# One-hot gate operands in an expert-retrieval kernel: made dense, token by token, by compare-and-scale instructions instead of for four interleaved tokens at once

## The chip, the core and the metric

The kernel runs on one core of a Trainium2 chip. Five engines work side by side, each with an in-order queue: TensorE (PE in the profile; its weight loads are listed as PEld), VectorE (DVE), ScalarE (ACT), GpSimd (POOL) and SyncE (SP, which issues the DMAs). They wait for each other through semaphores. The metric is the device time of one execution in microseconds (us); less is better.

## What is computed

The model is a decoder trunk of two layers on 256 tokens of width 1024. Each layer has a token-mixing sublayer (recurrent, state-space and attention heads; not touched here) and an expert retrieval, which is the place of the change. For each token, eight heads each choose 16 of 128 x 128 = 16384 experts; an expert is a pair of keys (i, j) and has a softmax gate. The output is the gated sum of the chosen experts:

```python
idx = jnp.take_along_axis(cand_i.reshape(c, PEER_HEADS, -1), best_pos, axis=-1)
gate = jax.nn.softmax(best_s, axis=-1)
ue = u[idx]
ve = v[idx]
act = jax.nn.gelu(jnp.einsum('td,thkd->thk', xc, ue).astype(jnp.float32), approximate=False)
return jnp.einsum('thk,thkd->td', (gate * act).astype(xc.dtype), ve)
```

## The kernel before

The kernel does not gather experts. It multiplies the tokens with all 16384 rows of u (the *first product*), applies GeLU, multiplies by a gate that is zero for the experts not chosen, and multiplies with all rows of v (the *second product*). The weights stream from HBM in pieces of 128 x 1024 floats. Each piece is split into a high half `hi` by ACT (line 117) and a low half `lo` by DVE, or for about every third piece of u by POOL (line 118), and every product is made of three matmuls: hi x hTh, hi x hTl, lo x hTh. All matmuls outside the transposes are issued by the helper `mm`, so they stand on line 193 in the profile; they are told apart by their tiles.

In `peer`, the loop over `jp_` (64 rounds, two pieces of u each) does the first product into the PSUM tile `acc`, 24 matmuls of 256 columns for one piece (columns are tokens). Between the pieces, `bg.step` advances background work that is written as Python generators: first `routing` for the two halves of the tokens, which finds the chosen keys and leaves them as `ijT` (key numbers i and j, in half floats) and `gT` (the gate as a high and a low half float); partition = choice (head and rank, 128 of them), column = token. Then `wgen` runs, one group of TG = 4 tokens for one piece of u, 64 groups for a layer. In a step it calls `gates` for group g, `wmm` for group g - 1 and `apply` for group g - 2.

`gates` makes the operands of a group on DVE in three instructions. Line 937 compares a constant ramp with the keys i and j of four tokens (`eq`, 1024 elements a partition). Line 940 multiplies the i half by the two gate halves (the first two planes of `ga`). Line 942 scales the j half for the low plane (the third plane of `ga`). The four tokens are the innermost dimension of these tiles, so the 128 elements that belong to one token lie four elements apart. `wmm` then makes the dense 128 x 128 gate matrix of each token from two half-float matmuls of 128 columns, 8 matmuls for a group. `apply` puts the gates onto `act`: for the experts whose first product is already there by a multiplication on DVE (line 956), for the others by a copy on ACT (line 958). `uevac` (lines 977 to 980) takes each finished `acc` through GeLU.

The order of instructions on each engine is fixed when the program is built, by a scheduler that goes by its own estimate of when operands are ready; on the chip each engine then follows its list. `eq` and `ga` have two buffers each. All of this happens twice, once per layer; in the first layer the groups are worked on from about 431 to 677 us, in the second from about 1474 to 1720 us.

Of the kernel before, what the change touches and what calls it, by code (L numbers as in the profile page):

```python
# [10 lines left out]
F16 = mybir.dt.float16  # L11
U32 = mybir.dt.uint32
AF = mybir.ActivationFunctionType
OP = mybir.AluOpType
AX = mybir.AxisListType

D = 1024
# [29 lines left out]
def trunk(ctx, tc, x, wst, ut, vr, pp_d, rb_d, lnrow, bd_d, keys_d, out):  # L47
    nc = tc.nc
    PE, ACT, DVE, POOL, SP = nc.tensor, nc.scalar, nc.vector, nc.gpsimd, nc.sync

    const = ctx.enter_context(tc.tile_pool(name="const", bufs=1))
    hpool = ctx.enter_context(tc.tile_pool(name="hpool", bufs=1))
    stream = ctx.enter_context(tc.tile_pool(name="stream", bufs=1))
    psum = ctx.enter_context(tc.tile_pool(name="psum", bufs=1, space=bass.MemoryType.PSUM))
    dram = ctx.enter_context(tc.tile_pool(name="dram", bufs=1, space=bass.MemoryType.DRAM))

# [1 line left out]
    items = []  # L58
    index = {}

# [70 lines left out]
    def rawtile(key):  # L131
        n = index[key]
        pump_dma()
        return raws[n]

    def rawdone(key):
        n = index[key]
        raws.pop(n)
        done.add(n)
        pump_dma()  # L140


# [1 line left out]
    mixp = tc.tile_pool(name="mix0", bufs=1)  # L144
    mix = mixp.__enter__()
    jp = mix.tile([128, 128], F32, name="jp")
    POOL.iota(jp, pattern=[[1, 128]], base=0, channel_multiplier=-1, allow_small_or_imprecise_dtypes=True)
    ident = const.tile([128, 128], F32, name="ident")
    POOL.tensor_scalar(ident, jp, 0.0, None, op0=OP.is_equal)
    iota4 = const.tile([128, 128, 4], F16, name="iota4")  # L150
    iota16 = const.tile([128, 16, 16], BF16, name="iota16")
    identb = const.tile([128, 128], BF16, name="identb")
    tri_le = const.tile([128, 128], F32, name="tri_le")
# [14 lines left out]
        return rb[:, l, o:o + w]  # L168

    def make_consts():  # L170
        POOL.iota(iota4, pattern=[[1, 128], [0, 4]], base=0, channel_multiplier=0, allow_small_or_imprecise_dtypes=True)
        POOL.iota(iota16, pattern=[[1, 16], [0, 16]], base=0, channel_multiplier=0, allow_small_or_imprecise_dtypes=True)
        POOL.tensor_scalar(identb, jp, 0.0, None, op0=OP.is_equal)
        POOL.tensor_scalar(tri_le, jp, 0.0, None, op0=OP.is_ge)
        POOL.tensor_scalar(tri_gt, jp, 0.0, None, op0=OP.is_lt)
        POOL.tensor_scalar(tri_gr, jp, 0.0, None, op0=OP.is_lt)
        for i in range(4):
            POOL.tensor_scalar(mask0[:, i, :], jp, 0.0, NEG, op0=OP.is_gt, op1=OP.mult)
        for i in range(2):
            POOL.tensor_scalar(mask1[:, i, 0, :], jp, 0.0, NEG, op0=OP.is_le, op1=OP.mult)  # L180
            POOL.tensor_scalar(mask1[:, i, 1, :], jp, 0.0, NEG, op0=OP.is_gt, op1=OP.mult)
# [10 lines left out]
    def mm(ps, lhsT, rhs, start, stop):  # L192
        PE.matmul(ps, lhsT, rhs, start=start, stop=stop)  # L193
# [4 lines left out]
    def acc_bank():  # L198
        return psum.tile([128, 512], F32, name="acc", bufs=4)

# [1 line left out]
    def layer_norm(h, pool, pre, gb, store, nxt=None, final=False, after=None):  # L202
        """h [128, 2, D] in place, stored to store; returns the transposed split operands."""
        ring = isinstance(gb[0], tuple)
        g, b = (rawtile(k) for k in gb) if ring else gb
        with tc.high_priority():
            hT = layer_norm_(h, pool, pre, g, b, store, nxt and index[nxt], final, after)
        for k in gb if ring else ():
            rawdone(k)
        return hT  # L210
# [93 lines left out]
    def seq(t):  # L304
        return [(w[0],) + tuple(int(ch) for ch in w[1:]) for w in t.split()]

    # (step, token block, part): r residual and sums, m mean and squares, v variance, n reciprocal root, s centre and
    # gain, o scale and bias with the transposes, l low halves, p the next weight pieces
    LN_ORDER = (
        seq("r00 r01 m0 v0 s00 s01 n00 r10 n01 r11 n02 m1 n03 v1 o00 o01 s10 n10 s11 n11 l00 n12 p1 n13 o10 o11 l01 l10 l11 p2"),  # L310
        seq("r00 r01 m0 s00 s01 v0 r10 n00 r11 n01 m1 n02 n03 o00 v1 o01 s10 n10 s11 n11 n12 n13 p1 o10 o11 l00 l01 l10 l11 p2"),
        seq("r00 r01 m0 s00 s01 v0 n00 n01 n02 r10 n03 r11 m1 s10 s11 v1 o00 n10 o01 n11 n12 n13 o10 o11"))

# [1 line left out]
    class Background:  # L315
        def __init__(self):
            self.q = []
# [39 lines left out]
        return y  # L357

    def log1p_exp_neg_abs(pool, o, xin, n, tag):
        """o = max(x, 0) + log1p(exp(-|x|)) on [128, n]"""  # L360
        a = pool.tile([128, n], F32, name=tag + "_a")
        e = pool.tile([128, n], F32, name=tag + "_e")
        q = pool.tile([128, n], F32, name=tag + "_q")
        ACT.activation(a, xin, AF.Abs)
        ACT.activation(e, a, AF.Exp, scale=-1.0)
        DVE.tensor_scalar(a, e, 2.0, None, op0=OP.add)
        DVE.reciprocal(a, a)
        DVE.tensor_tensor(e, e, a, op=OP.mult)
        DVE.tensor_tensor(a, e, e, op=OP.mult)
        DVE.tensor_scalar(q, a, 1.0 / 17.0, None, op0=OP.mult)  # L370
        for c in (15, 13, 11, 9, 7, 5, 3):
            DVE.scalar_tensor_tensor(q, q, 1.0 / c, a, op0=OP.add, op1=OP.mult)
        DVE.scalar_tensor_tensor(q, q, 1.0, e, op0=OP.add, op1=OP.mult)
        DVE.tensor_scalar(o, xin, 0.0, None, op0=OP.max)
        DVE.scalar_tensor_tensor(o, q, 2.0, o, op0=OP.mult, op1=OP.add)

# [1 line left out]
    def layer_consts(l, mix):  # L378
        av = mix.tile([128, 16], F32, name="av")
        sp4 = mix.tile([128, 4], F32, name="sp4")  # L380
        sp8 = mix.tile([128, 4], F32, name="sp8")
        sp2 = mix.tile([128, 4], F32, name="sp2")
        hba = mix.tile([128, 8], F32, name="hba")
        lamn = mix.tile([128, 4], F32, name="lamn")
        ACT.activation(av, RB("alog", l), AF.Exp)
        DVE.tensor_scalar(lamn, P("lam", l, 0, 4), -1.0, None, op0=OP.mult)
        log1p_exp_neg_abs(mix, sp8, lamn, 4, "lm")
        DVE.tensor_scalar(sp2, sp8, 2.0, None, op0=OP.mult)
        DVE.tensor_scalar(sp4, sp8, -4.0, None, op0=OP.mult)
        DVE.tensor_scalar(hba, P("rba", l, 0, 8), 0.5, None, op0=OP.mult)  # L390
        return av, sp2, sp4, hba

    def mixer(l, mix, h, hT, pre):
# [3 lines left out]
        yTl = mix.tile([128, 16, SEQ], F32R, name="yTl")  # L397
        xs = mix.tile([128, N_XBC, SEQ], F32, name="xs")

        # small per-layer values  # L400
        dt = mix.tile([128, 2, 16], F32, name="dt")
        da = mix.tile([128, 2, 16], F32, name="da")
        das = mix.tile([128, 2, 2, 16], F32R, name="das")
# [25 lines left out]
            yield  # L429
            yield  # L430

        # causal depthwise convolution
        def conv(o, xp, w0, bias=None):
            if bias is None:
                DVE.tensor_scalar(o, xp[:, 0:SEQ], w0(0), None, op0=OP.mult)
# [157 lines left out]
        ii = mix.tile([128, 4, SEQ], F32, name="ii")  # L593
# [129 lines left out]
                stages[st_](*units[u])  # L723
                yield

        # projection schedule
        order = [8, 9, 10, 11, 0, 1, 2, 3, 4, 5, 6, 7]
        for n, blk in enumerate(order):
            ps = bank([128, SEQ])
# [5 lines left out]
            if n == 3:  # L735
                ps = bank([128, SEQ])
# [8 lines left out]
        for blk in range(4):  # L745
            ps = bank([128, SEQ])
# [6 lines left out]
        for blk in range(4):  # L753
            ps = bank([128, SEQ])
# [5 lines left out]
        for i in range(6):  # L760
            ps = bank([128, SEQ])
# [7 lines left out]
        for nh in range(2):  # L769
            pz = [acc_bank() for _ in range(2)]  # L770
            for kp in range(4):
                hi, lo = weights(("w", l, n0 + nh * 4 + kp))
                for kk in range(2):
                    k = kp * 2 + kk
                    cs = slice(kk * 512, (kk + 1) * 512)
                    for tb in range(2):
                        ts = slice(tb * 128, (tb + 1) * 128)
# [6 lines left out]
                ACT.activation(sz[:, tb, nh * 512:(nh + 1) * 512], pz[tb], AF.Silu)  # L784
        n0 += N_Z
        bg.add(ssm_final())
        # output projection
        po = [[acc_bank() for _ in range(2)] for _ in range(2)]
        oorder = list(range(0, 16))
        def out_mm(i, kb, w, tb):  # L790
# [26 lines left out]

    RA, RB2, RX = 2, 2, 1

# [1 line left out]
    def peer(l, pool, hT):  # L821
        hTh, hTl = hT
        act = pool.tile([128, 128, SEQ], F32, name="act")
        ijT = pool.tile([128, 2, SEQ], F16, name="ijT")
        gT = pool.tile([128, 2, SEQ], F16, name="gT")
# [5 lines left out]
        for hh in range(8):  # L831
            ps = bank([128, SEQ])
# [3 lines left out]
        for tb in range(2):  # L836
            for hp in range(4):
                ps = bank([128, 2, 256])
# [13 lines left out]
        def routing(tb):  # L852
            base = 92
# [13 lines left out]
            gr = view(base + 7, 1)[:, 128:256]  # L867
# [37 lines left out]
            ts = slice(tb * 128, (tb + 1) * 128)  # L905
            for i in range(2):
# [9 lines left out]
                ps = bank([128, 128])  # L916
# [4 lines left out]
            ps = bank([128, 128])  # L921
# [1 line left out]
            yield  # L923
            ACT.activation(gT[:, 0, ts], ps, AF.Copy, scale=GS)
            DVE.scalar_tensor_tensor(gr, ps, GS, gT[:, 0, ts], op0=OP.mult, op1=OP.subtract)
            ACT.activation(gT[:, 1, ts], gr, AF.Copy, scale=LS)
            yield

        state = dict(c=0, t=0)
        TG = 4  # L930
        GS, LS = float(2 ** 15), float(2 ** 11)

        def gates(t0):
            eq = pool.tile([128, 2, 128, TG], F16, name="eq", bufs=2)
            A = pool.tile([128, 3, 128, TG], F16, name="ga", bufs=2)
            sh = [128, 2, 128, TG]
            DVE.tensor_tensor(eq, iota4[:, None, :, :].to_broadcast(sh),  # L937
                              ijT[:, :, None, t0:t0 + TG].to_broadcast(sh), op=OP.is_equal)
            # gate = (hi + lo / LS) / GS in half floats
            DVE.tensor_tensor(A[:, 0:2], eq[:, 0:1].to_broadcast(sh), gT[:, :, None, t0:t0 + TG].to_broadcast(sh),  # L940
                              op=OP.mult)
            DVE.tensor_scalar(A[:, 2], eq[:, 1], 1.0 / LS, None, op0=OP.mult)  # L942
            return A, eq

        def wmm(A, eq):
            ps = bank([128, TG, 128])
            for i in range(TG):
                mm(ps[:, i, :], A[:, 0, :, i], eq[:, 1, :, i], True, False)
                mm(ps[:, i, :], A[:, 1, :, i], A[:, 2, :, i], False, True)
            return ps  # L950

        def apply(t0, ps):
# [34 lines left out]
        for jp_ in range(64):  # L987
            ps = psum.tile([128, 2, SEQ], F32, name="acc", bufs=4)
# [3 lines left out]
            uevac(jp_, ps)  # L992
        bg.drain()

        # second product
        po = [[acc_bank() for _ in range(2)] for _ in range(2)]
        early = [[pool.tile([128, w], F32R, name=nm, bufs=2)[:, 0:2 * SEQ] for _ in range(2)]
                 for nm, w in (("eq", 512), ("ga", 768))]
# [37 lines left out]
                v_mm(j, w, tb)  # L1036
        return po

# [1 line left out]
    h = mix.tile([128, 2, D], F32, name="h")  # L1040
    gb = mix.tile([128, 2, D], F32, name="y")
    for i in range(2):
# [8 lines left out]
    for l in range(DEPTH):  # L1051
# [12 lines left out]
        h = mix.tile([128, 2, D], F32, name="h")  # L1064
# [85 lines left out]
```

## Time and profile before

| | |
|---|---|
| time, median of 3 runs | 2103.36 us (2100.47 to 2103.9) |
| profiled execution, first to last instruction | 2106.6 us |
| PE, PEld busy | 2030.2 us (96%), 1835.5 us (87%) |
| DVE busy | 1548.2 us (73%) |
| ACT, POOL busy | 1062.8 us (50%), 238.3 us (11%) |
| mean granted TensorE clock | 0.991 of full speed |
| DMA | 344.84 MB, 164 GB/s |

The profiled execution is not one of the three timed runs: the profile gives its own time as its span, 2106.6 us, and no other. Busy shares are averages over stages in which different engines set the pace, so the stage of the change has to be looked at by itself. A busy PE in this profile means that some matmul was in flight; since matmuls overlap, the distance from one start to the next tells more than a duration.

### The profile page before, as it was taken

The page shows a single profiled execution, that of the slowest core. Times are in us where ns is not written, and L with a number is a line of the kernel's source. Part 1 is how long each engine was busy: PE and PEld are TensorE (multiplying, and loading weights), DVE is VectorE, ACT ScalarE, POOL GpSimd, SP SyncE. Part 2 cuts the span into 40 slices and gives each one's busy share as a digit, 9 for nine tenths or more (in the row PEclk, how much of TensorE's full clock was granted, in tenths as well). Part 3 has the DMA queues.
Part 4 walks back from the last instruction along what each step waited for, and adds up shares of the span by engine and source line. Part 5 has one row for each costly group of instructions (what it writes and reads, how often), then busy time and mean ns, then how long its engine had stood idle before and what let it go on. Part 6 is the DMA issues. An engine that isn't in the chain of part 4 may idle for free. (4 is left out here: it accounts for less than half of the span.)

```text
span 2106.6 us, 33808 instructions
## 1 busy us (share of the span) xinstructions
PE 2030.2 (96%) x13212; PEld 1835.5 (87%) x13212; DVE 1548.2 (73%) x2713; ACT 1062.8 (50%) x1523; POOL 238.3 (11%) x120
## 2 busy tenths in 40 slices
PE   7999889999999999999989999899999999999998
PEld 6887889999999888888888769899999998888886
DVE  8786697379999655555687867963999995555555
ACT  5576455454443544444566755554444344444444
POOL 3100122222220000000010001222222200000000
PEclk9999999999999999999999999999999999999999
DMA  6434445544434666666654335455444446666665
GB/s 206 136 110 150 152 152 168 180 141 140 132 130 135 195 194 194 192 194 195 197 180 139 108 133 170 155 173 174 140 132 134 136 151 190 193 196 192 195 195 170
DMA packets 95919, 344.84 MB, mean 164 GB/s; under 512 B 11680, under 2 KB 11952, under 8 KB 95760
## 3 DMA queue, kind: packets, MB, share of 16 engines
q1 hardware_dynamic: 95552, 342.27, 50.3%
q8 instruction: 103, 1.69, 0.3%
q0 software_dynamic: 208, 0.42, 0.1%
q14 instruction: 56, 0.46, 0.1%
HBM read 339.51 MB, written 3.15 MB: 163 GB/s over the span
## 5 line engine op out<-in xcount | busy, mean ns | idle before, releaser
L118 DVE TENSOR_TENSOR lo<-raw,hi 128x1024 fp32r<-128x1024 f32 x544 | 677.5, 1246 | 383.9 <-ACT hi L117 383.5
L117 ACT ACTIVATE hi<-raw 128x1024 fp32r<-128x1024 f32 x630 | 663.8, 1056 | 452.2 <-PE acc L193 342.5
L193 PE MATMUL acc<-hTh,lo 128*128 128x256 f32 x2048 | 581.8, 284 | 20.1 <-DVE lo L118 18.8
L193 PE MATMUL acc<-hTh,hi 128*128 128x256 f32 x2048 | 592.0, 289 | 0.2 <-ACT hi L117 0.2
L193 PE MATMUL acc<-hTl,hi 128*128 128x256 f32 x2048 | 580.1, 283 | 0.0
L193 PEld LDWEIGHTS acc<-hTh,lo 128*128 128x128 f32 x2048 | 392.1, 191 | 24.3 <-DVE lo L118 22.4
L193 PE MATMUL acc<-hi,hTl 128*128 128x512 f32 x1056 | 411.4, 390 | 0.0
L193 PE MATMUL acc<-hi,hTh 128*128 128x512 f32 x1056 | 411.2, 390 | 0.0
L193 PE MATMUL acc<-lo,hTh 128*128 128x512 f32 x1056 | 411.1, 389 | 0.0
L193 PEld LDWEIGHTS acc<-hTh,hi 128*128 128x128 f32 x2048 | 394.3, 193 | 0.7 <-ACT hi L117 0.4
L193 PEld LDWEIGHTS acc<-hTl,hi 128*128 128x128 f32 x2048 | 392.8, 192 | 0.1
L118 POOL TENSOR_TENSOR lo<-raw,hi 128x1024 fp32r<-128x1024 f32 x86 | 223.6, 2602 | 1046.7 <-ACT hi L117 1015.7
L193 PEld LDWEIGHTS acc<-hi,hTh 128*128 128x128 f32 x1056 | 198.3, 188 | 41.6 <-issue 0.7
L193 PEld LDWEIGHTS acc<-hi,hTl 128*128 128x128 f32 x1056 | 198.2, 188 | 41.1
L193 PEld LDWEIGHTS acc<-lo,hTh 128*128 128x128 f32 x1056 | 198.3, 188 | 41.1
L193 PE MATMUL w<-hTh,hi 128*128 128x256 f32 x560 | 161.4, 299 | 7.5 <-DVE y L495 5.7
L1011 ACT ACTIVATE hTh<-act 128x512 fp32r<-128x512 f32 x124 | 77.7, 631 | 166.2 <-PE acc L193 166.2
L1012 DVE TENSOR_TENSOR hTl<-act,hTh 128x512 fp32r<-128x512 f32 x124 | 85.4, 693 | 97.4 <-ACT hTh L1011 97.4
L193 PE MATMUL w<-hTh,lo 128*128 128x256 f32 x560 | 156.9, 289 | 0.0
L193 PE MATMUL w<-hTl,hi 128*128 128x256 f32 x560 | 155.4, 287 | 0.0
L958 ACT ACTIVATE act<-w 128x272 f32<-128x272 f32 (+32 forms) x128 | 61.1, 478 | 146.5 <-DVE act L956 145.8
L193 PE MATMUL w<-eq,ga 128*128 128x128 f16 x512 | 128.0, 294 | 6.9 <-DVE ga L940 6.9
(268 smaller groups left out, 2323.5 us busy)
## 6 DMA issues: line engine op xcount, KB each, us to landing
raw<-in_ut SPq DMA_DIRECT2D x256, 512.0 KB, 3.5
raw<-in_vr SPq DMA_DIRECT2D x256, 512.0 KB, 3.5
raw<-in_wst SPq DMA_DIRECT2D x118, 512.0 KB, 3.5
raw<-in_lnrow SPq DMA_DIRECT2D x8, 512.0 KB, 3.6
hd<-h SPq DMA_DIRECT2D x4, 512.0 KB, 3.9
raw<-hd SPq DMA_DIRECT2D x4, 512.0 KB, 3.5
h<-in_x SPq DMA_DIRECT2D x2, 512.0 KB, 5.7
y<-in_lnrow SPq DMA_DIRECT2D x2, 512.0 KB, 7.0
```

Of the source, the lines that this page charges most:

```text
L117: ACT.activation(hi, raw, AF.Copy)
L118: (POOL if n in on_pool else DVE).tensor_tensor(lo, raw, hi.bitcast(F32), op=OP.subtract)
L193: PE.matmul(ps, lhsT, rhs, start=start, stop=stop)
L958: ACT.activation(v[:, :, c:128], ps[:, :, c:128], AF.Copy, scale=1.0 / GS)
L1011: ACT.activation(gh, src, AF.Copy)
L1012: DVE.tensor_tensor(gl, src, gh.bitcast(F32), op=OP.subtract)
```

## The change

`gates` now loops over the four tokens of a group. For each token it makes one row of `eq` (the key j) and two rows of `ga` (the key i, scaled by the high and by the low half of the gate), each 128 elements that lie side by side, and each by one tensor-scalar instruction on DVE. The instruction compares the ramp with a key that it reads per partition and, for `ga`, multiplies by a gate half that it reads per partition. The ramp shrinks from 512 to 128 elements, the scale `LS` of the low half goes, and with it the third plane of `ga`. `wmm` issues as many matmuls as before, on the dense rows. The other lines of the diff remove comments, so that later lines have numbers that are one less.

```diff
-    iota4 = const.tile([128, 128, 4], F16, name="iota4")
+    iota1 = const.tile([128, 128], F16, name="iota1")
...
-        POOL.iota(iota4, pattern=[[1, 128], [0, 4]], base=0, channel_multiplier=0, allow_small_or_imprecise_dtypes=True)
+        POOL.iota(iota1, pattern=[[1, 128]], base=0, channel_multiplier=0, allow_small_or_imprecise_dtypes=True)
...
-            ACT.activation(gT[:, 1, ts], gr, AF.Copy, scale=LS)
+            ACT.activation(gT[:, 1, ts], gr, AF.Copy)
...
         def gates(t0):
-            eq = pool.tile([128, 2, 128, TG], F16, name="eq", bufs=2)
-            A = pool.tile([128, 3, 128, TG], F16, name="ga", bufs=2)
-            sh = [128, 2, 128, TG]
-            DVE.tensor_tensor(eq, iota4[:, None, :, :].to_broadcast(sh),
-                              ijT[:, :, None, t0:t0 + TG].to_broadcast(sh), op=OP.is_equal)
-            DVE.tensor_tensor(A[:, 0:2], eq[:, 0:1].to_broadcast(sh), gT[:, :, None, t0:t0 + TG].to_broadcast(sh),
-                              op=OP.mult)
-            DVE.tensor_scalar(A[:, 2], eq[:, 1], 1.0 / LS, None, op0=OP.mult)
+            eq = pool.tile([128, TG, 128], F16, name="eq", bufs=2)
+            A = pool.tile([128, TG, 2, 128], F16, name="ga", bufs=2)
+            for i in range(TG):
+                ii, jj = (ijT[:, c, t0 + i:t0 + i + 1] for c in range(2))
+                DVE.tensor_scalar(eq[:, i, :], iota1, jj, None, op0=OP.is_equal)
+                for c in range(2):
+                    DVE.tensor_scalar(A[:, i, c, :], iota1, ii, gT[:, c, t0 + i:t0 + i + 1], op0=OP.is_equal, op1=OP.mult)
             return A, eq
 
         def wmm(A, eq):
             ps = bank([128, TG, 128])
             for i in range(TG):
-                mm(ps[:, i, :], A[:, 0, :, i], eq[:, 1, :, i], True, False)
-                mm(ps[:, i, :], A[:, 1, :, i], A[:, 2, :, i], False, True)
+                for c in range(2):
+                    mm(ps[:, i, :], A[:, i, c, :], eq[:, i, :], c == 0, c == 1)
             return ps
```

The next two lists are DVE's order in the middle of the first layer's groups, around the two multiplications by the gates (`apply`) that cover 78 experts a token; `iota_78` is the ramp. Before:

```order
L937 TENSOR_TENSOR eq<-iota_78,ijT 128x1024
L118 TENSOR_TENSOR lo<-raw,hi 128x1024
L978 TENSOR_TENSOR act<-act,acc 128x2x92
L940 TENSOR_TENSOR ga<-eq,gT 128x1024
L942 TENSOR_SCALAR ga<-eq 128x512
L956 SCALAR_TENSOR_TENSOR act<-w,act 128x4x78
L937 TENSOR_TENSOR eq<-iota_78,ijT 128x1024
L118 TENSOR_TENSOR lo<-raw,hi 128x1024
L940 TENSOR_TENSOR ga<-eq,gT 128x1024
L942 TENSOR_SCALAR ga<-eq 128x512
L956 SCALAR_TENSOR_TENSOR act<-w,act 128x4x78
```

And at the same place after the change:

```order
L118 TENSOR_TENSOR lo<-raw,hi 128x1024
L977 TENSOR_TENSOR act<-act,acc 128x2x92
L939 TENSOR_SCALAR eq<-iota_78,ijT 128x128
L941 TENSOR_SCALAR ga<-iota_78,ijT,gT 128x128 x2
L939 TENSOR_SCALAR eq<-iota_78,ijT 128x128
L941 TENSOR_SCALAR ga<-iota_78,ijT,gT 128x128 x2
L939 TENSOR_SCALAR eq<-iota_78,ijT 128x128
L941 TENSOR_SCALAR ga<-iota_78,ijT,gT 128x128 x2
L939 TENSOR_SCALAR eq<-iota_78,ijT 128x128
L941 TENSOR_SCALAR ga<-iota_78,ijT,gT 128x128 x2
L955 SCALAR_TENSOR_TENSOR act<-w,act 128x4x78
L118 TENSOR_TENSOR lo<-raw,hi 128x1024
```

Between two `apply` steps there are now twelve instructions with one or two per-partition operands where there were three without any; the split of a weight piece, the multiplication after GeLU and `apply` keep their places between the groups.

On PE the same stretch is, before, a block of eight gate matmuls between the 24 matmuls of one piece and those of the next (its last rows here):

```order
L193 LDWEIGHTS ga
L193 MATMUL w<-eq,ga 128x128
L193 LDWEIGHTS ga
L193 MATMUL w<-ga 128x128
L193 MATMUL acc<-hTh,hi 128x256
L193 MATMUL acc<-hTl,hi 128x256
L193 MATMUL acc<-hTh,lo 128x256
```

And after the change:

```order
L193 LDWEIGHTS ga
L193 MATMUL w<-eq,ga 128x128
L193 MATMUL acc<-hTh,hi 128x256
L193 LDWEIGHTS ga
L193 MATMUL w<-eq,ga 128x128
L193 MATMUL acc<-hTl,hi 128x256
L193 MATMUL acc<-hTh,lo 128x256
L193 MATMUL acc<-hTh,hi 128x256
L193 LDWEIGHTS ga
L193 MATMUL w<-eq,ga 128x128
```

From about the eighteenth group of a layer on, the gate matmuls are scattered singly between those of the first product. Of the first product's 3072 matmuls in a layer, 216 come after the last gate matmul, where it was 240: 24 matmuls, one piece of u, more are done by then.

## Rows read from the trace of the kernel before

**Rows 1.** The page: its first line, the span.

```profile
span 2106.6 us, 33808 instructions
```

**Rows 2.** Windows: start:end length, PE, PEld, DVE, ACT, POOL busy (count), clock, DMA, GB/s.

```profile
431.00:677.00 246.00, 242.26 (x2016) 237.32 (x2014) 234.82 (x323) 108.12 (x186) 48.52 (x18) 1.00 0.41 134
1474.00:1720.00 246.00, 242.86 (x2024) 238.12 (x2022) 234.46 (x323) 108.51 (x186) 49.36 (x18) 1.00 0.41 135
```

**Rows 3.** Groups by line, DVE, 431 to 685 us: busy us, mean ns, idle before.

```profile
L940 DVE TENSOR_TENSOR ga<-eq,gT 128x1024 f16<-128x1024 f16 x62 | 61.2, 987 | 0.9
L937 DVE TENSOR_TENSOR eq<-iota,ijT 128x1024 f16<-128x1024 f16 x62 | 56.8, 916 | 2.7 <-PE w L193 2.6
```

**Rows 4.** Waits of DVE and PE, 431 to 685 us: total us, times, longest.

```profile
DVE lo L118 <- ACT hi L117: 7.1, 7, 1.2
DVE act L956 <- ACT act L980: 2.8, 9, 0.5
DVE eq L937 <- PE w L193: 2.6, 3, 1.5
...
PE w L193 <- DVE ga L940: 3.7, 6, 0.9
```

**Rows 5.** Timeline of DVE (start us, us): the three instructions of a gate group.

```profile
446.17 0.70 DVE L940 TENSOR_TENSOR ga<-eq,gT 128x1024 f16<-128x1024 f16 x1
446.77 0.30 DVE L942 TENSOR_SCALAR ga<-eq 128x512 f16<-128x512 f16 x1
446.98 0.72 DVE L956 SCALAR_TENSOR_TENSOR act<-w,act 128x232 f32<-128x232 f32 x1
447.59 0.69 DVE L937 TENSOR_TENSOR eq<-iota,ijT 128x1024 f16<-128x1024 f16 x1
448.19 0.70 DVE L956 SCALAR_TENSOR_TENSOR act<-w,act 128x232 f32<-128x232 f32 x1
```

**Rows 6.** Timeline of PE: strided gate matmuls; dense bf16 matmuls in the routing.

```profile
457.09 0.28 PE L193 MATMUL acc<-hTh,lo 128*128 128x256 f32 x1
457.21 0.28 PE L193 MATMUL w<-eq,ga 128*128 128x128 f16 x1
...
461.03 0.29 PE L193 MATMUL w<-eq,ga 128*128 128x128 f16 x1
...
343.88 1.07 PE L193 MATMUL w<-identb,act 128*128 128x128 bf16 x16
344.78 0.28 PE L922 MATMUL w<-ident,act 128*128 128x128 f32 x1
```

**Rows 7.** Tensor-scalar lines: ns min/median/max; last, a timeline row.

```profile
L942 DVE TENSOR_SCALAR ga<-eq x128: 231/282/325, 352.9 to 1718.9; 128x512 f16<-128x512 f16 x128
L897 DVE TENSOR_SCALAR act<-act x4: 198/207/216, 288.4 to 1381.8; 128x128 f32<-128x128 f32 x4
L623 DVE TENSOR_SCALAR aa<-rr x4: 418/420/422, 107.8 to 1166.6; 128x512 f32<-128x512 f32 x4
L573 DVE TENSOR_SCALAR y<-y,rs_y x8: 481/482/487, 167.4 to 1213.3; 128x512 f32<-128x512 f32 x8
L435 DVE TENSOR_SCALAR xs<-xp,pp x24: 341/348/2503, 24.7 to 1108.5; 128x256 f32<-128x256 f32 x24
L437 DVE TENSOR_SCALAR xc<-xp,pp x8: 404/408/2500, 67.7 to 1123.0; 128x256 f32<-128x256 f32 x8
...
167.35 1.68 DVE L573 TENSOR_SCALAR y<-y,rs_y 128x512 f32<-128x512 f32 x4
```

**Rows 8.** POOL by line, 431 to 685 us; a DVE timeline row under one.

```profile
L118 POOL TENSOR_TENSOR lo<-raw,hi 128x1024 fp32r<-128x1024 f32 x18 | 48.5, 2695 | 163.2 <-ACT hi L117 152.8 <-PE acc L193 10.4
...
459.03 2.71 DVE L940 TENSOR_TENSOR ga<-eq,gT 128x1024 f16<-128x1024 f16 x1
```

**Rows 9.** Window behind a lull of PE (columns of rows 2); PE's timeline row.

```profile
337.00:341.00 4.00, 4.00 (x23) 4.00 (x24) 2.96 (x7) 1.77 (x1) 0.00 (x0) 0.61 0.82 256
...
336.78 0.58 PE L193 MATMUL acc<-hTh,lo 128*128 128x256 f32 x1 [2.08 <-DVE lo L118]
```

More of the change, by code (lines that the diff above doesn't have):

```diff
@@ L930, in peer @@
         TG = 4
-        GS, LS = float(2 ** 15), float(2 ** 11)
+        GS = float(2 ** 15)
         def gates(t0):
-            eq = pool.tile([128, 2, 128, TG], F16, name="eq", bufs=2)
-            A = pool.tile([128, 3, 128, TG], F16, name="ga", bufs=2)
-            sh = [128, 2, 128, TG]
-            DVE.tensor_tensor(eq, iota4[:, None, :, :].to_broadcast(sh),
-                              ijT[:, :, None, t0:t0 + TG].to_broadcast(sh), op=OP.is_equal)
-            DVE.tensor_tensor(A[:, 0:2], eq[:, 0:1].to_broadcast(sh), gT[:, :, None, t0:t0 + TG].to_broadcast(sh),
-                              op=OP.mult)
-            DVE.tensor_scalar(A[:, 2], eq[:, 1], 1.0 / LS, None, op0=OP.mult)
+            eq = pool.tile([128, TG, 128], F16, name="eq", bufs=2)
[5 more added lines that the diff above has]
+                    DVE.tensor_scalar(A[:, i, c, :], iota1, ii, gT[:, c, t0 + i:t0 + i + 1], op0=OP.is_equal, op1=OP.mult)
             return A, eq
```

## The prediction

> **What bounds the kernel now.** The sum is made against the profiled execution, whose own time is its span, 2106.6 us [rows 1]. The three timed runs have a median of 2103.36 us, 3.2 us less; what the change adds is worked out on the profiled execution and put on the median. A measurement of this kernel can tell about 0.2% (4 us) from no change.
>
> I read the windows first, by stage. The stage of the change is 431 to 677 us in the first layer and 1474 to 1720 us in the second. In these 246 us PE is busy for 242 and DVE for 235 [rows 2]: two engines at their limit at once, while ACT (108) and POOL (49) have room. Both layers agree within 0.6 us, so one is worked out and doubled. The view of waits says how near the two are: from 431 to 685 us DVE waits 7.1 + 2.8 + 2.6 = 12.5 us in all, for the high halves, for the GeLU and for PE; PE waits 3.7 us, always for the gate operands from DVE [rows 4]. PE sets the pace, but DVE has only about 12.5 us a layer, or 0.20 us for each of the 62 groups made in the stage, before it does.
>
> In PE's timeline one round (8 gate matmuls and the 24 matmuls of one piece of u) takes 461.03 - 457.21 = 3.82 us. A matmul of the first product starts 0.12 us after the one before, so 24 take 2.88 and the 8 gate matmuls about 0.94, or 0.118 each [rows 6].
>
> **What is removed.** On DVE, per group, 62 times a layer: in the timeline the step from the start of the `ga` product to the next instruction is 0.60 us, that of the small scaling 0.21, that of `eq` 0.60 [rows 5]. Together 1.41 us. Their mean durations are longer (987 and 916 ns, where the timeline shows 700 and 690) because a part of them is stretched to 2.7 us, which is treated below [rows 3, 5, 8].
>
> **What is added.** Twelve tensor-scalar instructions of 128 dense half floats: four with one per-partition operand (`eq`), eight with two (`ga`). None like them is in the trace, so I build the price from three differences between tensor-scalar lines [rows 7].
> - Size. With an immediate scalar, 512 half floats take 282 ns, 512 floats 420 ns and 128 floats 207 ns. The floats cost (420 - 207) / 384 = 0.55 ns each; 512 half floats at half of that would take 207 - 128 x 0.55 + 512 x 0.277 = 279 ns, and 282 were measured. So 128 dense half floats take about 282 - 384 x 0.277 = 176 ns. The next instruction starts some 0.08 to 0.09 us before the end (0.30 long, step 0.21 [rows 5]); I take a step of 0.10 us.
> - One per-partition operand. The line that scales 512 floats by such an operand takes 482 ns, the one with an immediate 420: 62 ns more. It isn't hidden back to back either: four in a row take 1.68 us, which is (1.68 - 0.48) / 3 = 0.40 us a step for what lasts 0.48 us, the same 0.08 us of overlap.
> - Two. The convolution's first tap with one such operand takes at least 341 ns, the one with a second (the bias) at least 404: 63 ns more.
>
> So `eq` steps by 0.10 + 0.062 = 0.162 us and `ga` by 0.10 + 0.062 + 0.062 = 0.224 us. A group costs 4 x 0.162 + 8 x 0.224 = 2.44 us instead of 1.41: 1.03 us more, and 62 x 1.03 = 64 us more in the stage. Bounds: from below, per-partition operands for nothing, 12 x 0.10 = 1.20 us a group; from above, half floats of this size at the rate of floats, 0.033 us more each, 2.84 us a group. The operands differ from the priced ones in type (half floats, not floats) and in nothing that the rows show to matter, so I take 2.44.
>
> [...]
>
> **On PE.** As many gate matmuls as before. The routing's dense matmuls of the same 128 columns step by (344.78 - 343.88) / 16 = 0.056 us, against 0.118 for the strided ones [rows 6]. Where a gate matmul now stands alone between two of the first product, the following weight load must fit behind it, and it may keep 0.118. So a round costs PE between 3.33 and 3.82 us. DVE's round, without waits, is (246 - 12.5) / 62 = 3.77 us now and 3.77 + 1.03 = 4.80 us then. DVE becomes the bound by far, PE waits at the gate matmuls, and what PE gains is worth nothing.
>
> **The sum.** Per layer: +64 on DVE. As DVE becomes the late one, most of its 12.5 us of waiting goes; I take 8 of them (bounds 0 and 12.5). PE does one more piece of u before the last gate matmul, so 24 x 0.12 = 2.9 us less remain behind. 64 - 8 - 2.9 = 53 us, and for two layers 106 us. The first two groups of a layer are made before the stage, where PE is never short of work; DVE's extra 2 us there are covered by its idle time before the following `lo`, and if they weren't, 4 us in all would be added. The shorter ramp (POOL, at the start) and the missing scale on ACT are off any path. 2103.4 + 106 = 2209 us on the median, 2213 us on a span.
>
> **The rivals.**
> - *Per-partition operands cost nothing* in this form. Then a group costs DVE 1.20 us, 0.2 us or 13 us a layer less than now, and PE's round shrinks too; the stage would lose 10 to 20 us a layer: about 2073 us, faster. The point from which it decides is the mean step of the twelve: below 1.41 / 12 = 0.118 us DVE gains, and up to about 0.134 its 0.20 us of waiting a group covers the rest. For it: no row shows this operand type. Against: each row with such an operand shows the 62 ns, and my mean step is 0.203. Chance 6%.
> - *The second operand comes with the first.* Twelve steps of 0.162 make 1.94 us, 0.53 more a group, 33 a layer; 33 - 8 - 2.9 = 22, twice 44: about 2148 us. Against it stands the one pair of lines with 341 and 404 ns. Chance 10%.
> - *Port and clock make it worse.* POOL runs 18 splits a layer in the stage, 2.7 us each, and a DVE instruction that reads two SBUF tiles under one is stretched to 2.7 us [rows 8]. The excess over 0.68 us comes to 62 x (0.987 - 0.684) + 62 x (0.916 - 0.684) = 33 us a layer, 1.8 for each of the 18 [rows 3]. One-input lines are stretched as well (maxima of 2503 and 2500 ns [rows 7]), so the twelve are exposed as much as the three were; with DVE never pausing, the loss may grow to the whole of POOL's time, 0.5 to 0.9 us each, 9 to 16 us a layer. [...] Together 15 to 25 us a layer on top: 2240 to 2260 us. Chance 16%. [...]
> - *Half floats at the rate of floats.* 0.40 us more a group, 25 a layer: about 2259 us. Chance 5%.
>
> **How the numbers follow.** The forecast has the rest, 63%, and a range of its own of 2190 to 2235 (all or none of the waits absorbed: 2200 to 2225; and 0.07 us a group either way in the price). The range of 2148 to 2265 reaches down to the second rival and up to the worse cases; left out are the first rival, half of the second's lower side and what goes above. Faster comes from the first rival alone, 6%; no change needs a mean step just at 0.118 to 0.134 us, 2%; slower has 92%.
>
> **What the changed profile would show.** Right: tensor-scalar lines of about 0.24 us (`eq`) and 0.30 us (`ga`), steps near 0.16 and 0.22; a stage of about 300 us a layer in which DVE is busy nearly all the time and PE no longer; PE's waits on the gate operands grown from 4 to 60 us or more a layer; gate matmuls in blocks stepping by 0.056 us; nothing changed outside. Wrong: steps of 0.10 for both (first rival), equal steps for `eq` and `ga` (second), PE's clock below 1.00 in the stage or DVE's stretched time well above 33 us a layer (third).

## The result and the profile after

The changed kernel takes 2222.82 us (median of 4 runs, 2220.63 to 2224.28) against 2103.57 us for the kernel before (4 runs on the same chip, 2100.47 to 2103.9): a ratio of 1.0568, interval 1.0553 to 1.0583, slower. That is 119 us; the profiled executions differ by 111.8 us, from 2106.6 [rows 1] to 2218.4 us. The 7 us between the two lie within the scatter of single executions: a timed execution is some 2 us longer than its span (2220.63 against 2218.4 for the same one), so the profiled execution of before is about 5 us above its median, and over all the runs of this study the kernel before ran from 2098 to 2114 us.

The page of the changed kernel, span and busy time; DVE has 138 us more than before, PE 37 us more:

```profile
span 2218.4 us, 34972 instructions
...
PE 2067.6 (93%) x13210; PEld 1827.2 (82%) x13212; DVE 1685.7 (76%) x3865; ACT 1066.2 (48%) x1523; POOL 227.1 (10%) x120
```

Its windows over the two stages, in the columns of [rows 2]:

```profile
431.00:735.00 304.00, 266.21 (x2047) 238.69 (x2045) 301.10 (x882) 111.82 (x189) 44.07 (x18) 0.94 0.34 110
1530.00:1833.00 303.00, 264.09 (x2048) 236.73 (x2046) 300.42 (x881) 111.67 (x188) 42.91 (x18) 0.95 0.34 111
```

The stage has grown from 246 to 304 us and DVE is busy for 301 of them. PE, busy for 242 of 246 before, has 38 us to spare, and its clock is below full speed, which it wasn't before. All of the added time is here: the last gate matmul of the first layer starts at 734.55 us (677.49 before); the first of the second layer at 1530.24 (1473.72); the last at 1833.47 (1719.96). So 57 us come in each stage, and little is added or given back between them.

The two new lines over the whole run (nanoseconds: least, median, longest), in the columns of [rows 7]:

```profile
L939 DVE TENSOR_SCALAR eq<-iota,ijT x512: 235/241/2426, 349.0 to 1832.2; 128x128 f16<-128x128 f16 x171
L941 DVE TENSOR_SCALAR ga<-iota,ijT,gT x1024: 257/301/2489, 349.1 to 1832.5; 128x128 f16<-128x128 f16 x171
```

And the same two in the first layer's stage, the groups that take the place of [rows 3]:

```profile
L941 DVE TENSOR_SCALAR ga<-iota,ijT,gT 128x128 f16<-128x128 f16 x496 | 147.4, 336 | 0.0
L939 DVE TENSOR_SCALAR eq<-iota,ijT 128x128 f16<-128x128 f16 x248 | 78.8, 318 | 1.1 <-PE w L193 1.1
```

DVE's waits in the stage, as [rows 4], have gone from 12.5 to 3.5 us:

```profile
DVE act L955 <- ACT act L979: 1.2, 2, 0.6
DVE act L977 <- ACT act L957: 1.2, 1, 1.2
DVE eq L939 <- PE w L193: 1.1, 1, 1.1
```

PE's waits have gone from 3.7 to 38.6 us:

```profile
PE w L193 <- DVE ga L941: 25.4, 29, 2.2
PE acc L193 <- DVE lo L118: 13.2, 19, 1.0
```

DVE's timeline through one group, which answers to [rows 5]:

```profile
446.47 0.24 DVE L939 TENSOR_SCALAR eq<-iota,ijT 128x128 f16<-128x128 f16 x1
446.63 0.52 DVE L941 TENSOR_SCALAR ga<-iota,ijT,gT 128x128 f16<-128x128 f16 x2
447.08 0.23 DVE L939 TENSOR_SCALAR eq<-iota,ijT 128x128 f16<-128x128 f16 x1
447.24 0.52 DVE L941 TENSOR_SCALAR ga<-iota,ijT,gT 128x128 f16<-128x128 f16 x2
447.69 2.33 DVE L939 TENSOR_SCALAR eq<-iota,ijT 128x128 f16<-128x128 f16 x1
449.94 0.52 DVE L941 TENSOR_SCALAR ga<-iota,ijT,gT 128x128 f16<-128x128 f16 x2
```

A token takes 447.08 - 446.47 = 0.61 us, which is 0.16 for `eq` and 0.45 for two rows of `ga`. The medians of all steps are 0.163 and 0.223 us, so a group costs 2.44 us. The row of 2.33 us is an `eq` under one of POOL's splits, which runs from 447.56 us for 2.40 us.

PE's timeline, to be read beside [rows 6], a block of gate matmuls early in the stage and single ones later:

```profile
437.34 0.62 PE L193 MATMUL w<-eq,ga 128*128 128x128 f16 x8
437.77 0.36 PE L193 MATMUL acc<-hTh,hi 128*128 128x256 f32 x1
...
570.33 0.23 PE L193 MATMUL w<-eq,ga 128*128 128x128 f16 x1
570.37 0.36 PE L193 MATMUL acc<-hTh,hi 128*128 128x256 f32 x1
570.58 0.23 PE L193 MATMUL w<-eq,ga 128*128 128x128 f16 x1
```

In a block the eight take 0.43 us, about 0.055 each, where they took 0.118. A single one and the matmul behind it take 570.58 - 570.33 = 0.25 us, where the latter alone takes 0.12; the median over the 339 single ones of the first layer is 0.242 us. So a lone gate matmul costs about 0.12 us, as much as a strided one did. The weight load that follows it starts at 570.33 us as well and takes 0.20 us.

### The profile page after: what moved, and what is told of

The parts are those of the page before. It is cut to its first block, busy times and chain, and to the rows that moved or that the text cites. A ratio compares the mean times of both kernels' runs of the same rounds, so it can differ in the third digit from the quotient of the medians.

```text
span 2218.4 us, 34972 instructions
## 1 busy us (share of the span) xinstructions
PE 2067.6 (93%) x13210; PEld 1827.2 (82%) x13212; DVE 1685.7 (76%) x3865; ACT 1066.2 (48%) x1523; POOL 227.1 (10%) x120
## 5 line engine op out<-in xcount | busy, mean ns | idle before, releaser
L193 PE MATMUL acc<-hTh,lo 128*128 128x256 f32 x2048 | 616.1, 302 | 48.8 <-DVE lo L118 46.9
L193 PE MATMUL acc<-hTh,hi 128*128 128x256 f32 x2048 | 614.8, 301 | 0.5 <-ACT hi L117 0.5
L193 PE MATMUL acc<-hTl,hi 128*128 128x256 f32 x2048 | 606.9, 297 | 0.0
L193 PEld LDWEIGHTS acc<-hTh,lo 128*128 128x128 f32 x2048 | 406.7, 199 | 62.5 <-DVE lo L118 60.3
L193 PEld LDWEIGHTS acc<-hTh,hi 128*128 128x128 f32 x2048 | 407.6, 199 | 0.8 <-ACT hi L117 0.7
L193 PEld LDWEIGHTS acc<-hTl,hi 128*128 128x128 f32 x2048 | 407.1, 199 | 0.1
L941 DVE TENSOR_SCALAR ga<-iota,ijT,gT 128x128 f16<-128x128 f16 x1024 | 309.8, 341 | 0.0
L193 PE MATMUL w<-eq,ga 128*128 128x128 f16 x1024 | 199.6, 232 | 52.2 <-DVE ga L941 52.1
L193 PEld LDWEIGHTS <-ga 128*128 128x128 f16 x1024 | 89.7, 98 | 98.5 <-DVE ga L941 62.6
L939 DVE TENSOR_SCALAR eq<-iota,ijT 128x128 f16<-128x128 f16 x512 | 157.7, 308 | 2.2 <-PE w L193 2.2
```

Of the source, the lines that this page charges most:

```text
L939: DVE.tensor_scalar(eq[:, i, :], iota1, jj, None, op0=OP.is_equal)
L941: DVE.tensor_scalar(A[:, i, c, :], iota1, ii, gT[:, c, t0 + i:t0 + i + 1], op0=OP.is_equal, op1=OP.mult)
```

## The experiments

Ten kernels were run. The theory of the prediction is that DVE becomes the bound and that the price is that of the per-partition operands, 0.062 us each. The rivals are that the number of instructions, the scattered matmuls or POOL's splits make the time, and that the second operand is free.

**No per-partition operand.** From the changed kernel:

```diff
-                DVE.tensor_scalar(eq[:, i, :], iota1, jj, None, op0=OP.is_equal)
+                DVE.tensor_scalar(eq[:, i, :], ijT[:, 1, hs], 5.0, None, op0=OP.is_equal)
-                    DVE.tensor_scalar(A[:, i, c, :], iota1, ii, gT[:, c, t0 + i:t0 + i + 1], op0=OP.is_equal, op1=OP.mult)
+                    DVE.tensor_scalar(A[:, i, c, :], gT[:, c, hs], 5.0, 2.0, op0=OP.is_equal, op1=OP.mult)
```

> From the changed kernel, twelve instructions a group as there, on as many dense half floats, but with immediate constants instead of the per-partition key and gate half (the ramp is replaced by a window of the keys or gates, so the real gates are left out). Theory (the per-partition operands are the cost, 0.062 us each): both lines step by 0.10 us, a group costs 1.20 us, DVE is 0.2 us a group lighter than in the kernel before and PE is the bound again, with a round of 3.3 to 3.8 us: 2060 to 2100 us, faster than before. Rival (the number of instructions, the scattered gate matmuls or the port are the cost): the steps may shrink, but the time stays at 2200 us or above.

Measured: 2096.85 us, ratio to before 0.9973 (0.996 to 0.9986). DVE's timeline:

```profile
442.22 0.19 DVE L939 TENSOR_SCALAR eq<-ijT 128x128 f16<-128x128 f16 x1
442.32 0.29 DVE L941 TENSOR_SCALAR ga<-gT 128x128 f16<-128x128 f16 x2
442.52 0.19 DVE L939 TENSOR_SCALAR eq<-ijT 128x128 f16<-128x128 f16 x1
442.62 0.29 DVE L941 TENSOR_SCALAR ga<-gT 128x128 f16<-128x128 f16 x2
442.83 0.67 DVE L955 SCALAR_TENSOR_TENSOR act<-w,act 128x224 f32<-128x224 f32 x1
```

All twelve step by 0.10 us (0.30 us a token), and the whole loss is gone with as many instructions as in the changed kernel. The rival that counts instructions falls. The rival of the scattered matmuls isn't tested here, for in this kernel all gate matmuls stand in blocks of eight again. The time lies at the upper end of what was expected, because other waits grow: in the first stage DVE waits 13.7 us for the high halves (7.1 before [rows 4]), and PE still 9.2 us for `ga`, by the view of waits:

```profile
DVE lo L118 <- ACT hi L117: 13.7, 14, 1.2
...
PE w L193 <- DVE ga L941: 9.2, 15, 1.2
```

**One operand instead of two** in the rows of `ga`:

```diff
-                    DVE.tensor_scalar(A[:, i, c, :], iota1, ii, gT[:, c, t0 + i:t0 + i + 1], op0=OP.is_equal, op1=OP.mult)
+                    DVE.tensor_scalar(A[:, i, c, :], gT[:, c, hs], ii, 2.0, op0=OP.is_equal, op1=OP.mult)
```

> From the changed kernel; eq as there (one per-partition operand), the two rows of ga with one per-partition operand (the key) and a constant in place of the gate half (the real gates are left out). Theory (each operand costs its own 0.062 us): ga steps by 0.16 instead of 0.223 us, a group costs 1.94 instead of 2.44 us, 31 us a layer less while DVE is the bound: about 2160 us. Rival (one charge for reading operands at all, the second comes with the first): no change against the changed kernel, 2223 us.

Measured: 2157.41 us, ratio 1.0263 (1.0246 to 1.028). DVE's timeline:

```profile
442.34 0.25 DVE L940 TENSOR_SCALAR eq<-iota,ijT 128x128 f16<-128x128 f16 x1
442.50 0.41 DVE L942 TENSOR_SCALAR ga<-gT,ijT 128x128 f16<-128x128 f16 x2
442.83 0.25 DVE L940 TENSOR_SCALAR eq<-iota,ijT 128x128 f16<-128x128 f16 x1
```

A token takes 0.49 us, three equal steps of 0.163. So the ladder is 0.102, 0.163 and 0.223 us for none, one and two operands, and one operand less in the eight rows of `ga` is worth 65 us over both layers (57 by the profiled executions; by the steps 62 x 8 x 0.06 x 2 = 60). The rival of the free second operand falls.

**Dense operands alone.** The kernel before with its DVE instructions; the matmuls read dense blocks of the same tiles:

```diff
+            Af, ef = (x.rearrange("p c k t -> p (c k t)") for x in (A, eq))
-                mm(ps[:, i, :], A[:, 0, :, i], eq[:, 1, :, i], True, False)
-                mm(ps[:, i, :], A[:, 1, :, i], A[:, 2, :, i], False, True)
+                b0, b1 = i * 256, i * 256 + 128
+                mm(ps[:, i, :], Af[:, b0:b0 + 128], ef[:, 512 + i * 128:640 + i * 128], True, False)
+                mm(ps[:, i, :], Af[:, b1:b1 + 128], Af[:, 1024 + i * 128:1152 + i * 128], False, True)
```

> From the kernel before, its three DVE instructions kept as they are; the gate matmuls read blocks of 128 neighbouring elements of the same tiles instead of elements four apart (they are the wrong elements, the right gates are left out). It is the dense half of the change alone. Theory (DVE has only about 0.2 us a group to spare, so it becomes the bound): gate matmuls step by 0.056 us, PE's round falls to 3.3 us, the stage loses only 5 to 12 us a layer: 2080 to 2095 us. Rival (PE alone is the bound): 0.49 us x 62 = 30 us a layer, about 2043 us. Second rival (scattered or not, a gate matmul keeps 0.118 us): 2103 us.

Measured: 2093.5 us, ratio 0.9955 (0.994 to 0.997). Its gate matmuls step by 0.056 us, PE is busy for 228 of the stage's 247 us, and what it saves it waits, on DVE. The first and the last of a group's eight gate matmuls, the window and the wait:

```profile
450.54 0.23 PE L193 MATMUL w<-eq,ga 128*128 128x128 f16 x1
...
450.94 0.22 PE L193 MATMUL w<-ga 128*128 128x128 f16 x1
```

```profile
431.00:678.00 247.00, 228.14 (x2075) 218.37 (x2074) 235.86 (x328) 109.43 (x192) 51.77 (x18) 1.00 0.42 137
```

```profile
PE w L193 <- DVE ga L940: 17.9, 21, 1.6
```

So DVE is the bound as soon as PE is faster. With DVE's instructions as they were before, what the change gives to PE is worth 9 us in all.

**Whose stride.** As the last one, but only one of the two operands is dense in each layer:

```diff
+                if l == 0:
+                    mm(ps[:, i, :], A[:, 0, :, i], ef[:, 512 + i * 128:640 + i * 128], True, False)
+                    mm(ps[:, i, :], A[:, 1, :, i], Af[:, 1024 + i * 128:1152 + i * 128], False, True)
+                else:
+                    mm(ps[:, i, :], Af[:, b0:b0 + 128], eq[:, 1, :, i], True, False)
+                    mm(ps[:, i, :], Af[:, b1:b1 + 128], A[:, 2, :, i], False, True)
```

> From the kernel before, DVE as it is. In the first layer the gate matmuls read dense blocks only for the eq side and stay four elements apart on the ga side of line 193's operands; in the second layer the other way round (wrong elements in both, the right gates are left out). It tells whose stride costs the 0.118 instead of 0.056 us. If the weights' stride is the cost, the layer with dense weights steps by 0.056 us and the other by 0.118; if the moving side's, the reverse; if either is enough, both keep 0.118 us and the time is that of before, 2103 us; if each costs a share, both lie between. A layer that gets 0.056 us loses what it loses with both dense, some 5 to 12 us.

Measured: 2099.37 us, ratio 0.9984 (0.9969 to 0.9998). PE's timeline, first layer and second:

```profile
451.20 0.22 PE L193 MATMUL w<-ga 128*128 128x128 f16 x1
451.26 0.22 PE L193 MATMUL w<-eq,ga 128*128 128x128 f16 x1
...
1496.50 0.30 PE L193 MATMUL w<-eq,ga 128*128 128x128 f16 x1
1496.61 0.30 PE L193 MATMUL w<-ga 128*128 128x128 f16 x1
```

With the moving operand (the key j) dense and the weights four elements apart the step is 0.056 us; the other way round it is 0.116 us. The weights' stride costs nothing here, the moving operand's is all of it.

**POOL's splits taken out of the stage**, from the changed kernel:

```diff
-        on_pool.update(index["u", l, j] for j in range(4, 110, 3))
+        on_pool.update(index["u", l, j] for j in range(4, 55, 3))
```

> From the changed kernel; POOL splits pieces of u only up to piece 54, that is none in the stage of the gates, and DVE does those 18 splits a layer instead. Theory (a part of DVE's added time is lost to POOL's splits: 37.7 us of stretched instructions a layer in the changed kernel): DVE gets 18 x 1.14 = 20.5 us of splits more and loses 37.7 us of stretching, 17 us a layer less: about 2189 us. Rival (the stretched time is not POOL's doing, or comes back elsewhere): 20 us a layer more, about 2264 us.

Measured: 2181.3 us, ratio 1.0348 (1.0311 to 1.0386), 41 us less than the changed kernel. The window of the first stage:

```profile
435.00:724.00 289.00, 261.64 (x2083) 231.23 (x2082) 289.00 (x904) 115.18 (x194) 0.00 (x0) 1.00 0.37 119
```

The groups of the two lines there:

```profile
L941 DVE TENSOR_SCALAR ga<-iota,ijT,gT 128x128 f16<-128x128 f16 x496 | 135.4, 323 | 0.0
...
L939 DVE TENSOR_SCALAR eq<-iota,ijT 128x128 f16<-128x128 f16 x247 | 64.8, 262 | 0.0
```

And PE's chief wait, 48 times, 0.9 us at most:

```profile
PE acc L193 <- DVE lo L118: 26.6, 48, 0.9
```

`eq` is not stretched any more (its longest instruction of the whole run takes 353 ns, 2426 in the changed kernel), and the mean of `ga`, 323 ns, is below its median of 339. DVE is busy for all 289 us, and PE's waits are short and its granted clock is 1.00. The stage is 20 us shorter a layer, near the 17 expected. POOL's splits are a part of the loss, then, and not the most of it: the kernel is still 3.5% slower than before. The rival of the scattered matmuls falls here: 435 of the first layer's 512 gate matmuls stand alone, more than in the changed kernel, and it is DVE that is never idle.

**The third plane alone**, from the kernel before:

```diff
-            DVE.tensor_scalar(A[:, 2], eq[:, 1], 1.0 / LS, None, op0=OP.mult)
-                mm(ps[:, i, :], A[:, 1, :, i], A[:, 2, :, i], False, True)
+                mm(ps[:, i, :], A[:, 1, :, i], eq[:, 1, :, i], False, True)
```

> From the kernel before, with the interleaved layout, strided matmuls and its two large instructions as they are; only the scale of the low gate half goes, and with it the third plane of ga and the small scaling, so that DVE steps 0.21 us a group less. It is the one part of the change that takes work from DVE. Theory (PE, with its round of 3.82 us, and DVE are both at the limit before): DVE's relief is worth only what DVE made PE wait, 3 to 4 us a layer: 2094 to 2100 us. Rival (DVE is the bound): 0.21 x 62 = 13 us a layer, 2077 us.

Measured: 2095.32 us, ratio 0.9955 (0.9941 to 0.9969): 8 us for both layers, what PE waited before. PE is then busy for all of the stage:

```profile
428.00:672.00 244.00, 244.00 (x2044) 240.55 (x2043) 228.44 (x266) 112.40 (x192) 48.85 (x18) 1.00 0.43 139
```

**A dense j half with tensor-tensor instructions**, from the last kernel; `iota1` is a ramp of 128:

```diff
+            DVE.tensor_tensor(eq[:, 0], iota4, ijT[:, 0, None, t0:t0 + TG].to_broadcast([128, 128, TG]), op=OP.is_equal)
+            if l == 0:
+                DVE.tensor_tensor(ej, iota1[:, None, :].to_broadcast([128, TG, 128]),
+                                  ijT[:, 1, t0:t0 + TG, None].to_broadcast([128, TG, 128]), op=OP.is_equal)
+            else:
+                DVE.tensor_tensor(ej.rearrange("p t k -> p k t"), iota4,
+                                  ijT[:, 1, None, t0:t0 + TG].to_broadcast([128, 128, TG]), op=OP.is_equal)
```

> From the kernel with two planes. The comparison is split in two tensor-tensor instructions of 512 elements: the i half stays interleaved (it goes into the weights of the gate matmuls), the j half (their moving operand) is written densely per token; ga is as before. In the first layer the j instruction walks along a token, with the key held over 128 elements; in the second it walks over the four tokens and writes each element 256 bytes after the one before. Theory (only the moving operand's stride costs PE): gate matmuls step by 0.056 us in both layers. On DVE the two instructions should step by 0.33 us each if 512 elements run at the rate of the 1024 before (0.60 us), and the j one by up to 0.6 us if its pattern halves the rate. At the full rate DVE has 0.15 us a group less to do than in the kernel before: 2075 to 2090 us; at half the rate 0.1 us more: 2105 to 2120 us.

Measured: 2209.37 us, ratio 1.0484 (1.0448 to 1.052), worse than either case of the expectation. The three comparisons, in the columns of [rows 7]:

```profile
L941 DVE TENSOR_TENSOR eq<-iota,ijT x128: 404/422/2424, 338.7 to 1819.0; 128x512 f16<-128x512 f16 x128
...
L943 DVE TENSOR_TENSOR eq<-iota,ijT x64: 673/682/708, 348.7 to 678.1; 128x512 f16<-128x512 f16 x64
...
L946 DVE TENSOR_TENSOR eq<-iota,ijT x64: 2437/2482/2562, 1394.4 to 1819.4; 128x512 f16<-128x512 f16 x64
```

The interleaved half steps by 0.33 us. With the key held along the token 512 elements take as long as 1024 did (step 0.60). Written 256 bytes apart they take 2.48 us (step 2.08), and the second layer, not the first, makes the loss: its gate matmuls span 342 us, those of the first 250. On PE both forms gave 0.056 us, as expected, so the loss is DVE's.

**Pairs of tokens.** Keys and gates of two tokens lie side by side, both large instructions keep 1024 elements, and a gate operand's elements are 4 bytes apart instead of 8:

```diff
+        ijT = pool.tile([128, SEQ // 2, 2, 2], F16, name="ijT")
+        gT = pool.tile([128, SEQ // 2, 2, 2], F16, name="gT")
...
+            eq = pool.tile([128, QT, 2, 128, 2], F16, name="eq", bufs=2)
+            A = pool.tile([128, QT, 2, 128, 2], F16, name="ga", bufs=2)
...
+                    mm(ps[:, i, :], A[:, q, c, :, k], eq[:, q, 1, :, k], c == 0, c == 1)
```

> The kernel with two planes, its operands stored for two interleaved tokens instead of four (the keys and gates of a pair of tokens lie side by side, so that eq and ga are one instruction of 1024 half floats each, as there). An element of a gate matmul's operand follows the one before by 4 bytes instead of 8. Theory (the 0.118 us a gate matmul is a matter of the moving operand's stride of 8 bytes, and 4 bytes are no worse than dense, as the moving floats of the first product, 4 bytes apart, suggest): 0.056 us, PE's round falls to 3.33 us, DVE's steps stay at 0.60 us, and DVE's 15.6 us a layer of idle time in the stage shrink: 8 to 12 us a layer less than with four tokens, 2072 to 2082 us. Rival (any stride but dense costs): 0.118 us still, 2095 us; a stride of 4 bytes might also cost in between.

Measured: 2074.39 us, ratio 0.9849 (0.9823 to 0.9874). PE's timeline:

```profile
452.98 0.63 PE L193 MATMUL w<-eq,ga 128*128 128x128 f16 x8
453.42 0.36 PE L193 MATMUL acc<-hTh,hi 128*128 128x256 f32 x1
```

The eight take 0.44 us, as dense ones do (0.43 in the changed kernel).

**Pairs, and no splits on POOL in the stage** (both edits together):

> The same, and POOL splits no pieces of u in the stage of the gates; DVE does those 18 a layer. Theory (with dense or nearly dense gate matmuls DVE is the bound, and POOL's splits cost it more in stretched instructions, 32 us a layer, than they take off it, 18 x 1.14 = 20.5): 12 us a layer less than with the splits on POOL, 2050 to 2062 us, unless PE's 3.33 us a round or the high halves from ACT take over, then 2060 to 2072. Rival (POOL's splits pay as long as DVE waits at all): 2090 to 2115 us.

Measured: 2047.36 us, ratio 0.973 (0.9714 to 0.9746), the fastest of all: 59 us under the kernel before on the same chip. The window of the first stage:

```profile
427.00:650.00 223.00, 221.78 (x2081) 218.48 (x2079) 217.13 (x285) 114.25 (x194) 0.00 (x0) 1.00 0.44 153
```

Its groups of `eq` and `ga` on DVE:

```profile
L942 DVE TENSOR_TENSOR eq<-iota,ijT 128x1024 f16<-128x1024 f16 x62 | 42.5, 685 | 5.9 <-PE w L193 5.1
L944 DVE TENSOR_TENSOR ga<-eq,gT 128x1024 f16<-128x1024 f16 x62 | 42.3, 682 | 0.0
```

The stage is 223 us long, where it was 246, and both engines are busy in nearly all of it: PE sets the pace again, with about 3.4 us a round. Set beside [rows 3], `eq` and `ga` have lost their stretched part (916 and 987 ns before).

**That last edit in the kernel before**, the splits alone:

> The kernel before, unchanged but for the 18 pieces of u a layer that POOL splits in the stage of the gates: DVE splits them. It tells whether the gain of that step in the last kernel stands by itself. Theory (before, PE with strided gate matmuls is the bound at 3.82 us a round, and DVE made it wait only 3.7 us a layer): DVE loses 33 us of stretching and gains 20.5 us of splits, but the time falls only by what PE waited, 3 to 4 us a layer: 2094 to 2100 us. Rival (the step pays by itself): 12 us a layer, 2078 us. Second rival (20 us more splits on DVE make it late somewhere): above 2103 us.

Measured: 2096.35 us, ratio 0.996 (0.9946 to 0.9974): 8 us. DVE has less to do, but PE is busy for 245 of 245 us:

```profile
428.00:673.00 245.00, 245.00 (x2053) 241.54 (x2051) 229.72 (x346) 114.65 (x192) 0.00 (x0) 1.00 0.43 139
```

So each relief of one engine alone, the third plane, dense matmuls or the splits, was worth 8 to 9 us, and together they are worth 59.

## Why the prediction was right

The forecast was 2209 us, 2148 to 2265; 2222.82 was measured, within the forecast's own narrower range too. The terms per layer, measured on the two profiled executions (by the medians the change is 60 us a layer instead of 56):

| term | predicted, us | measured, us |
|---|---|---|
| price of a group, 62 x (2.44 - 1.41) | +64 | +64 |
| DVE's waits absorbed | -8 | -9 |
| stretching by POOL's splits | 0 (9 to 16 in a rival) | +5 |
| `apply` shorter, 64 x (930 - 960 ns) | 0 | -2 |
| one piece of u more before the last gate matmul | -2.9 | -1.7 |
| sum | +53 | +56 |

*The price.* Steps of 0.162 and 0.224 us were forecast, 0.163 and 0.223 came. Three differences between lines of floats [rows 7] were enough for half floats. That the operand's type doesn't matter was the assumption in it, and the steps here agree with it: 0.060 to 0.061 us for an operand with half floats against 0.062 to 0.063 for a float. Doing without all per-partition operands brought the whole loss back, and doing without the second one of `ga` about half.

*The two kernels without POOL in the stage* show the price without POOL's splits: the twelve instructions take 62 x 4 x 0.163 + 62 x 8 x 0.223 = 151 us a layer, the three 62 x 1.41 = 87. From the first gate matmul of a layer to the last these kernels take 283 and 242 us, so 42 of the 64 us show; in the second PE sets the pace, and DVE stands idle for 15 of its 245 us.

*The waits and the tail.* A little more of DVE's waiting was absorbed than assumed, 9 of 12.5 us. The tail gave back less than 2.9 us: from the last gate matmul to the last matmul of the first product it was 28.8 us and is 27.1, and PE still waits 0.9 us for a `lo` there.

*Port and clock*, the third rival. No trace here shows a port; what the traces show is that DVE instructions under one of POOL's splits are stretched. The excess of the 18 stretched instructions rose from 33 to 38 us a layer, each taken against its line's median; by the rows of `eq` and `ga` alone it is 248 x (0.318 - 0.241) + 496 x (0.336 - 0.301) = 36 us. So the stretching added 5 us where the rival had 9 to 16. The rival's other half, the clock, which the prediction had set down as a sign against itself, came too: 0.94 in the stage, with stretches at 0.50 (452 to 455 us is one). But no run shows the 6 to 9 us a layer by which the rival's 15 to 25 exceed its 9 to 16: DVE waited 3.5 us in all, 1.1 of them for PE, so PE's slower stretches were covered. Removing the splits brought the clock back to 1.00, and the 20 us that this saved are accounted for by DVE alone: 37.7 of stretching and 2.4 of waits less, 18 x 1.14 = 20.5 of splits more.

*What was read wrongly* is PE's slack. 60 us or more of waits on the gate operands were forecast, which is 62 x (4.80 - 3.82) = 61, the slow end of PE's round; 38.6 came, 25.4 on them and 13.2 on `lo`. Most gate matmuls stand alone (339 of 512), but at 0.12 us each they cost what that slow end allows for, so they don't explain it. What the forecast left out of PE's round is the clock: a part of the stage ran at a granted clock of 0.50 (0.94 in the mean), with waits of up to 2.2 us between the matmuls, and PE got 304 x (1 - 0.94) = 18 us less work done (an estimate). That is most of the 22 us that are missing; the rest stays open. Since DVE was the bound, the time doesn't show it.

*The first rival* would not have given its 2073 us: with immediates 2097 were measured at the step of 0.10 us that it supposes, since waits for the high halves take over. Why the kernel with pairs, at the same 1.20 us a group on DVE, reaches 2074 stays open. In the first layer DVE waits 8.4 us for the high halves with pairs and 13.7 with immediates; the order of the instructions differs too.

## What to carry to other kernels

Price a small tensor-scalar instruction by its step and add each per-partition operand separately; at 128 half floats two of them more than doubled it here (0.223 us against 0.102), and one wide tensor-tensor instruction that made eight such rows in 0.60 us was cheaper than eight of them (8 x 0.223 = 1.78). When two engines are at their limit together, a change that relieves one by loading the other can lose, as here, and single reliefs look worthless (8 to 9 us each here) until both are relieved (59 us). Ask which operand needs the dense layout, and how dense: pairs took TensorE 0.44 us for eight gate matmuls, as the dense layout did (0.43), and cost VectorE nothing in `eq` (a median of 685 ns, 683 before).

## What the hardware showed unexpectedly

- With the elements of its moving operand 8 bytes apart, a half-float matmul of 128 columns stepped by 0.116 to 0.118 us, and at 4 bytes by 0.057 us, like dense (0.056); weights 8 bytes apart cost nothing (0.056 with a dense moving operand).
- A VectorE write of half floats 256 bytes apart took 2.48 us for 512 elements, where a write of neighbours took 0.42 us.
- The duration of an instruction isn't its cost. `eq` has a median of 241 ns in the changed kernel; without POOL's splits its mean is 262 ns although none is stretched (353 at most), and its step is 0.163 us in both.
- One split on POOL took about 2 us from VectorE in this stage (37.7 / 18) and saved it 1.14, the step of one `lo`.
